# A hybrid attention layer on one core: part of the down projection by Strassen's block product, and the feed-forward casts moved to ScalarE

## The chip, the cores and the metric

The kernel runs on one core of a Trainium2 chip. A core has TensorE (PE in the profile), which multiplies matrices into the banks of PSUM, and VectorE (DVE), ScalarE (ACT), GpSimd (POOL) and SyncE (SP), each with an instruction queue of its own that is worked off in order; they meet at semaphores. The metric is the time of one execution on the device, in microseconds (us); the time told is the median of several runs.

## The reference

One layer of a streaming encoder, for 512 prompt tokens and 32 sample tokens. What matters here is its end:

```python
x = x + mixed @ w_out                        # two attention mixers, gated, [T, 1024]
h = rmsnorm(x, n2)
u = h @ w_up                                 # [T, 5632], w_up [1024, 5632]
c = conv_b + conv_w[0]*u[t-2] + conv_w[1]*u[t-1] + conv_w[2]*u[t]    # per feature, over time
a, g = split(c, 2)                           # 2816 features each
x = x + (gelu(a) * g) @ w_down               # w_down [2816, 1024]
```

The new rows of the caches (keys, values, the last two rows of `u`) are outputs too. All is float32.

## The kernel before

Activations stand transposed: features on the 128 partitions, T = 544 tokens (512 and 32) as columns, in two halves of 272. PE works on a rounded format, so each float32 operand is split into a high part (a cast) and a low part (the operand less its high part), and a product is made of three matmuls into one bank: high x high, high x low, low x high (`triple`, L210). A matmul here has a 128x128 block of weights and 272 columns.

Weights come as tiles of 128x1024 (512 KB), eight blocks each, in the order of the list `sources`: 52 tiles of `w_in`, 8 of `w_out`, 44 of `w_up`, 22 of `w_down`. `prep` (L185) loads a tile, makes its high part on POOL (L193) and its low part on DVE (L194), with two buffers for each of the three; `weights()` has it done up to three tiles ahead, at a low priority for the scheduler.

The order of PE's work is that in which Python emits it: `Stream` keeps a clock of its own while it emits, and lets attention tasks in between the projections when their operands should be there. Which instruction stands where on the other engines, and small exchanges on PE, are decided by the framework's scheduler, which goes by priorities and by its own estimate of durations. So an instruction can stand far from where the code emits it.

The feed-forward part has two stages.

- Up projection: `conv` (L921) takes tiles in pairs, a value tile `i` and its gate tile `GT + i`. Each tile is 48 matmuls (8 blocks, 2 halves, 3 products). DVE takes each half out of its bank times the norm (L925), ACT and DVE make the convolution (L931, L932, L937), POOL keeps the last rows of each sequence (L928, L929) and mends the sample's first two tokens (L934, L935) by a small table `carry`, made once by POOL (L916 to L919). ACT makes the gelu (L945), DVE multiplies by the gate (L950), and `split` (L419) makes the high part on ACT (L420) and the low part on DVE (L421) of the 22 gated tiles.
- Down projection (loop at L970): for each of 8 output tiles, 22 row blocks x 2 halves x 3 matmuls into two banks, then DVE adds the residual `x1` (L984) and SP stores the tile (L988, the last one in two halves, L986).

`fp` is a pool of 39 buffers of 128x544 and `gp` one of 19; `psd` and `psa` are 3 and 5 banks of PSUM.

Of the kernel before, what the change touches and what calls it, by code (L numbers as in the profile page):

```python
# [30 lines left out]
B_BLK = 96               # sample keys of mixer B: 3 blocks of 96 (32 new, 256 cached)
LN_EXP = "natural_log_exp_and_others"

# tiles of w_in, 128 output features each
QA, KA, VA, QB, KB, VB, GA, GB = 0, 8, 10, 12, 20, 28, 36, 44

# columns of the packed per-feature vectors
# [101 lines left out]
def body(ctx, tc, a, o):  # L139
# [39 lines left out]
    for i in range(GT):  # L179
        sources += [a["w_up"][i], a["w_up"][GT + i]]  # L180
# [789 lines left out]
    for m in range(KC):  # L970
# [5 lines left out]
        for k, s in order:  # L976
# [6 lines left out]
            if k == GT - 1:  # L983
                V.tensor_tensor(y[:, c0:c0 + cn], ps[s][:, :cn], x1[m][:, c0:c0 + cn], ALU.add)  # L984
                if tail:
                    nc.sync.dma_start(out=o["y"][m, :, c0:c0 + cn], in_=y[:, c0:c0 + cn])  # L986
# [118 lines left out]
```

## Time and profile before

| | |
|---|---|
| median of 3 runs | 934.15 us (934.09 to 934.8) |
| profiled execution: span from the first to the last instruction | 931.9 us |
| busy in the span: PE, DVE, ACT, POOL | 905.8, 656.7, 445.1, 467.0 us |
| down projection on PE | about 796 to 928.7 us |

The profile shows one execution. It gives the span and no time of its own beside it; the runs were timed apart from it. Busy time of PE counts a matmul's whole passage, and matmuls overlap (0.288 us each, started every 0.125 us), so the pace is read from the starts.

### The profile page before, as it was taken

How to read it: one execution, taken by the hardware profiler on the slowest of the kernel's cores; microseconds unless marked ns; L12 is line 12 of the kernel's file. 1: busy time of each engine (PE TensorE's matmuls, PEld its weight loads, DVE VectorE, ACT ScalarE, POOL GpSimd, SP SyncE). 2: the span in 40 equal slices, each digit the busy share in tenths (PEclk: the TensorE clock that was granted, in tenths of full speed). 3: DMA queues.
4: the chain of work that ended last, by engine and by line, in shares of the span. 5: the costliest groups of instructions: out<-in, count | busy, mean ns of one | idle time of the engine just before them, and what ended most of it. 6: DMA issues, size and time to landing. Idle time of an engine off the chain costs nothing.

```text
span 931.9 us, 18669 instructions
## 1 busy us (share of the span) xinstructions
PE 905.8 (97%) x7181; PEld 891.7 (96%) x7181; DVE 656.7 (70%) x1243; ACT 445.1 (48%) x1103; POOL 467.0 (50%) x636
## 2 busy tenths in 40 slices
PE   7979999999999999999999999999999999999998
PEld 6878999989989999999999999999999999999998
DVE  7798867777988988989766568777777777422221
ACT  5667887778878687777672232222222222000000
POOL 5625548366777677766451146544555554311110
PEclk9999999999999999999999999999999999999999
DMA  6222123312344344334324222222222222333321
GB/s 220 89 91 83 52 95 99 103 59 83 109 145 128 98 138 128 127 110 125 107 86 169 89 70 91 91 91 91 91 84 80 87 92 91 107 103 103 113 90 40
DMA packets 39000, 94.35 MB, mean 101 GB/s; under 512 B 4832, under 2 KB 14336, under 8 KB 38912
## 3 DMA queue, kind: packets, MB, share of 16 engines
q1 hardware_dynamic: 38912, 93.17, 31.1%
q8 instruction: 56, 0.92, 0.4%
q14 instruction: 32, 0.26, 0.1%
HBM read 80.48 MB, written 7.10 MB: 94 GB/s over the span
## 4 chain that ended last, share of the span: by engine, by line
PE 78%; DVE 8%; ACT 3%; POOL 3%; issue 2%; DMA 0%; DVEq 0%; POOLq 0%; ACTq 0%
PE ps L80 75%; PE ps L84 3%; DVE q L436 1%; ACT p L475 1%; DVE w_lo L194 1%; DVE p L491 1%; POOL p L483 1%; DVE zn L412 1%; DVE s L244 1%; DVE t_b L309 1%; POOL t_sql L404 1%; DVE k L421 0%; POOL z L411 0%; DVE xl L317 0%; DMA k<-k 0%
## 5 line engine op out<-in xcount | busy, mean ns | idle before, releaser
L80 PE MATMUL ps<-xh,w_lo 128*128 128x272 f32 x1536 | 444.4, 290 | 5.9 <-DVE w_lo L194 5.8
L80 PE MATMUL ps<-xh,w_hi 128*128 128x272 f32 x1536 | 444.1, 291 | 3.4 <-ACT z L402 1.6
L80 PE MATMUL ps<-xl,w_hi 128*128 128x272 f32 x1536 | 444.2, 290 | 1.3 <-DVE xl L317 1.2
L80 PEld LDWEIGHTS ps<-xh,w_lo 128*128 128x128 f32 x1536 | 289.4, 189 | 7.6 <-DVE w_lo L194 7.0
L80 PEld LDWEIGHTS ps<-xh,w_hi 128*128 128x128 f32 x1536 | 289.7, 189 | 4.9 <-ACT z L402 1.9
L80 PEld LDWEIGHTS ps<-xl,w_hi 128*128 128x128 f32 x1536 | 289.8, 189 | 2.6 <-DVE xl L317 2.1
L193 POOL TENSOR_SCALAR w_hi<-w_raw 128x1024 fp32r<-128x1024 f32 (+2 forms) x128 | 137.5, 1074 | 288.8 <-PE ps L80 178.2
L194 DVE TENSOR_TENSOR w_lo<-w_raw,w_hi 128x1024 fp32r<-128x1024 f32 (+2 forms) x128 | 162.4, 1270 | 105.6 <-POOL w_hi L193 105.2
L80 PE MATMUL ps<-s,w_hi 128*128 128x272 f32 x960 | 180.6, 288 | 0.0
L80 PEld LDWEIGHTS ps<-s,w_hi 128*128 128x128 f32 x960 | 150.4, 188 | 0.0
L80 PE MATMUL ps<-s,w_lo 128*128 128x272 f32 x480 | 137.8, 288 | 0.0
L483 POOL TENSOR_SCALAR p<-p,rc 128x256 f32<-128x256 f32 (+3 forms) x128 | 74.5, 598 | 43.3 <-DVE rc L481 39.9
L80 PEld LDWEIGHTS ps<-s,w_lo 128*128 128x128 f32 x480 | 90.2, 188 | 0.0
L475 ACT ACTIVATE p<-p,nm 128x256 f32<-128x256 f32 (+3 forms) x128 | 65.4, 513 | 27.8 <-DVE nm L472 27.7
L925 DVE TENSOR_TENSOR u<-ps,rstd 128x272 f32<-128x272 f32 x88 | 38.2, 438 | 38.8 <-PE ps L80 38.2
L420 ACT CAST s<-s 128x544 fp32r<-128x544 f32 x30 | 19.4, 647 | 84.9 <-DVE s L950 81.5
L80 PE MATMUL ps<-k,q 128*128 128x256 f32 (+2 forms) x256 | 52.1, 308 | 3.3 <-DMA k<-k 1.6
L404 POOL TENSOR_TENSOR t_sql<-t_sq,t_sqh 128x272 fp32r<-128x272 f32 x52 | 52.6, 1011 | 3.7
L411 POOL TENSOR_TENSOR z<-z,t_y 128x272 f32<-128x272 f32 x52 | 42.6, 821 | 21.9 <-ACT t_y L306 19.9
L931 ACT ACTIVATE s<-u,cols 128x544 f32<-128x544 f32 x44 | 36.9, 842 | 34.0 <-DVE u L925 34.0
L945 ACT ACTIVATE s<-s 128x544 f32<-128x544 f32 x22 | 14.5, 658 | 75.5 <-DVE s L937 75.5
L403 POOL TENSOR_SCALAR t_sqh<-t_sq 128x272 fp32r<-128x272 f32 x52 | 29.9, 575 | 39.4 <-ACT t_sq L401 34.7
(129 smaller groups left out, 1340.9 us busy)
## 6 DMA issues: line engine op xcount, KB each, us to landing
w_raw<-in_w_in SPq DMA_DIRECT2D x50, 512.0 KB, 3.3
w_raw<-in_w_up SPq DMA_DIRECT2D x44, 512.0 KB, 3.2
w_raw<-in_w_down SPq DMA_DIRECT2D x22, 512.0 KB, 3.2
k<-k SPq DMA_DIRECT2D x40, 128.0 KB, 2.3
bias<-in_rel SPq DMA_DIRECT2D x16, 256.0 KB, 2.7
w_raw<-in_w_out SPq DMA_DIRECT2D x8, 512.0 KB, 3.3
s<-in_x SPq DMA_DIRECT2D x15, 272.0 KB, 5.6
out_vb<-s SPq DMA_DIRECT2D x8, 272.0 KB, 2.3
```

What stands on the lines that cost most here:

```text
L80: return self.nc.tensor.matmul(out, lhsT=lhsT, rhs=rhs, **kw)
L84: return self.nc.tensor.transpose(out, src, ident)
L193: G.tensor_scalar(hi[:, c], raw[:, c], 1.0, 1.0, ALU.mult, ALU.mult)
L194: V.tensor_tensor(lo[:, c], raw[:, c], rr(hi)[:, c], ALU.subtract)
L403: G.tensor_scalar(sqh, sq, 1.0, 1.0, ALU.mult, ALU.mult)
L404: G.tensor_tensor(sql, sq, rr(sqh), ALU.subtract)
L411: G.tensor_tensor(z, z, y, ALU.mult)
L420: nc.scalar.copy(dst_hi, src)
L475: act(p[:, sl], p[:, sl], AF.Exp, bias=nm[:, t:t + 1], accum_out=sm[:, t:t + 1])
L483: G.tensor_scalar(p[:, sl], p[:, sl], rc[:, t:t + 1], 1.0, ALU.mult, ALU.mult)
L925: V.tensor_tensor(u[:, 2 + c0:2 + c0 + cn], ps, rstd2[:, c0:c0 + cn], ALU.mult)
L931: act(c, u[:, 0:T], AF.Identity, scale=col("cw0", m), bias=col("cb", m))
```

## The change

Of the 22 row blocks of the down projection, 6 (blocks 16 to 21, `REST`) are multiplied as before, and first: their gated tiles are now the first that the up projection makes. The other 16 make 8 pairs (block j with block j + 8). For a pair of output tiles, the 2x2 blocks of weights and the 2x2 blocks of the pair's two gated tiles (each cut into its two halves of 272 columns) are multiplied in Winograd's form of Strassen's product, with 7 products for 8:

- `make_pair` builds the seven moving operands of a pair from the two gated tiles: four additions or subtractions of 272 columns on DVE, the high parts on ACT, the low parts on DVE. Five pairs (`EARLY`) are made while the up projection goes on, three after it. The operands lie in the buffers of `gp`, `fp` (now 50), and, once the up projection has read them, in those of its moving operand (`xh`, `xl`).
- `sums` builds the seven weight operands. One load of 128x1024 holds the weight blocks of two pairs (a unit); DVE makes the four sums of 256 columns (one instruction for two of them), ACT the high parts, DVE the low parts. There are 4 pairs of output tiles x 4 units = 16 loads.
- Each of the seven products gathers 8 row blocks in a bank of its own (4 units x 2 x 3 = 24 matmuls), and `leave` adds the seven banks into the four quarters of the two output tiles: one copy on ACT, nine operations on DVE, two on POOL. Stores are by quarters.
- The high part of every weight tile of `w_up` and `w_down` is made on ACT, no longer on POOL.

```diff
-    for i in range(GT):
+    ffn = len(sources)
+    gate_order = list(range(2 * PAIRS, GT)) + [j + e * PAIRS for j in range(PAIRS) for e in range(2)]
+    for i in gate_order:
         sources += [a["w_up"][i], a["w_up"][GT + i]]
-    sources += [a["w_down"][m] for m in range(GT)]
+    sources += [a["w_down"][m] for m in range(KC * REST // 8)]
...
-            G.tensor_scalar(hi[:, c], raw[:, c], 1.0, 1.0, ALU.mult, ALU.mult)
+            if n < ffn:
+                G.tensor_scalar(hi[:, c], raw[:, c], 1.0, 1.0, ALU.mult, ALU.mult)
+            else:
+                nc.scalar.copy(hi[:, c], raw[:, c])
...
-    fp = att.enter_context(tc.tile_pool(name="fp", bufs=39, reuse_waits="tile"))
+    fp = att.enter_context(tc.tile_pool(name="fp", bufs=50, reuse_waits="tile"))
...
+    def make_pair(v1, v2):
+        b11, b12, b21, b22 = (v[:, c:c + H] for v in (v1, v2) for c in (0, H))
+        t13, t24 = (fp.tile([128, T], F32, name="s") for _ in range(2))
+        first, *wide = home(), (home(), home()), (home(), home()), (home(), home())
+        nc.scalar.copy(first[:, :H], b11)
+        V.tensor_tensor(first[:, H:], b11, rr(first)[:, :H], ALU.subtract)
+        split(*wide[0], v2)
+        V.tensor_tensor(t13[:, :H], b11, b12, ALU.subtract)
+        V.tensor_tensor(t13[:, H:], b12, b22, ALU.subtract)
+        split(*wide[1], t13)
+        V.tensor_tensor(t24[:, :H], b22, t13[:, :H], ALU.add)
+        V.tensor_tensor(t24[:, H:], b21, t24[:, :H], ALU.subtract)
+        split(*wide[2], t24)
...
+    def sums():
+        for n in range(KC // 2 * UNITS):
+            raw = wp.tile([128, 1024], F32, name="w_raw", bufs=2)
+            load(raw, a["w_pair"][n])
+            wc, wd, wa, wb = (raw[:, 256 * e:256 * e + 256] for e in range(4))
+            s13, s24 = (fp.tile([128, 2, 256], F32, name="s") for _ in range(2))
+            s1, s3, s2, s4 = s13[:, 0], s13[:, 1], s24[:, 0], s24[:, 1]
+            V.tensor_tensor(s13, raw[:, 256:768].rearrange("p (e c) -> p e c", e=2),
+                            wc.unsqueeze(1).to_broadcast([128, 2, 256]), ALU.add)
+            V.tensor_tensor(s2, s1, wa, ALU.add)
+            V.tensor_tensor(s4, s2, wb, ALU.add)
+            for x in (wa, s2, s3, s1, wb, wd, s4):
+                w = fp.tile([128, 2, 256], F32R, name="s")
+                nc.scalar.copy(w[:, 0], x)
+                V.tensor_tensor(w[:, 1], x, rr(w)[:, 0], ALU.subtract)
+                ready.append(w)
+                yield
...
+    FACTORS = ("b11", "t2", "t3", "t1", "b21", "t4", "b22")
...
+            if e == 0:
+                nc.scalar.copy(p1, ps[0])
+                G.tensor_tensor(y11, y11, p1, add)
+            elif e == 1:
+                tt(v2, ps[1], p1, sub)
+                tt(y12, y12, v2, sub)
+            elif e == 2:
+                tt(v3, ps[2], v2, add)
+                tt(y22, y22, v3, add)
+                G.tensor_tensor(y21, y21, v3, add)
+            elif e == 3:
+                tt(y22, y22, ps[3], sub)
+                tt(y12, ps[3], y12, add)
+                store(1, 1)
+            else:
+                y, r, h = ((y11, 0, 0), (y21, 1, 0), (y12, 0, 1))[e - 4]
+                tt(y, ps[e], y, add)
+                store(r, h)
...
+        for u in range(UNITS):
+            for e, name in enumerate(FACTORS):
+                w = operand(nprod)
+                nprod += 1
+                for j in range(2):
+                    xh, xl = pairs[2 * u + j][name]
+                    ks = slice(128 * j, 128 * j + 128)
+                    first, last = (u, j) == (0, 0), (u, j) == (UNITS - 1, 1)
+                    mm(ps[e], lhsT=w[:, 0, ks], rhs=xh, start=first, stop=False)
+                    mm(ps[e], lhsT=w[:, 0, ks], rhs=xl, start=False, stop=False)
+                    mm(ps[e], lhsT=w[:, 1, ks], rhs=xh, start=False, stop=last)
+                if u == UNITS - 1:
+                    leave(e)
```

`operand(n)` runs `sums` up to ten operands ahead of product `n`. The change also reserves less of SBUF for DMA descriptors (`dynamic_dma_scratch_size=1024`), which makes room for the larger pool. Up to the feed-forward part the instructions of every engine stand in the order of before, apart from two zeroings on DVE, which now come near its start, and the place shown next.

POOL, near the start of the program: `s<-s` is the running sum of squares for the first norm, `ks_lo` the low part of a cached key tile, `w_hi<-w_raw` the high part of weight tiles. Before:

```order
L332 TENSOR_TENSOR s<-s 128x544 x3
L421 TENSOR_TENSOR ks_lo<-c_k,ks_hi 64x128 x2
L193 TENSOR_SCALAR w_hi<-w_raw 128x1024 x2
L403 TENSOR_SCALAR t_sqh<-t_sq 128x272
L404 TENSOR_TENSOR t_sql<-t_sq,t_sqh 128x272
```

and now:

```order
L342 TENSOR_TENSOR s<-s 128x544 x3
L926 TENSOR_TENSOR carry<-cols 128x44 x2
L431 TENSOR_TENSOR ks_lo<-c_k,ks_hi 64x128
L928 TENSOR_TENSOR t_c<-cols 128x44
L431 TENSOR_TENSOR ks_lo<-c_k,ks_hi 64x128
L927 TENSOR_TENSOR carry<-carry,cols 128x44 x2
L929 TENSOR_TENSOR carry<-carry,t_c 128x44
L201 TENSOR_SCALAR w_hi<-w_raw 128x1024 x2
```

The six instructions that make `carry` stood just ahead of the feed-forward part; they now stand ahead of the high parts of the third and fourth weight tile of `w_in`.

DVE, behind the end of the up projection: before, the last tile's convolution, gate and low part, then weight low parts and the two evictions of each output tile:

```order
L194 TENSOR_TENSOR w_lo<-w_raw,w_hi 128x1024
L932 SCALAR_TENSOR_TENSOR s<-u_8049,cols,s 128x544
L937 SCALAR_TENSOR_TENSOR s<-u_8049,cols,s 128x544
L950 TENSOR_TENSOR s<-s 128x544
L421 TENSOR_TENSOR s<-s 128x544
L194 TENSOR_TENSOR w_lo<-w_raw,w_hi 128x1024 x2
L984 TENSOR_TENSOR s<-ps,s 128x272 x2
```

Now, from the second to the third weight low part of the six blocks (the third is the last row; L967 to L971 and L431 make the operands of late pairs, L1055 is the eviction):

```order
L965 TENSOR_TENSOR xh_11205<-s,xh_11205 128x272
L970 TENSOR_TENSOR s<-s 128x272
L967 TENSOR_TENSOR s<-s 128x272
L968 TENSOR_TENSOR s<-s 128x272
L942 SCALAR_TENSOR_TENSOR s<-u_8049,cols,s 128x544
L431 TENSOR_TENSOR xh_11167<-s,xl_11166 128x544
...
L1055 TENSOR_TENSOR s<-ps,s 128x272
L431 TENSOR_TENSOR xl_11188<-s,xh_11187 128x544
L947 SCALAR_TENSOR_TENSOR s<-u_8049,cols,s 128x544
L204 TENSOR_TENSOR w_lo<-w_raw,w_hi 128x1024
```

The weight low parts, which came back to back with the evictions, now have the late pairs' work between them.

DVE, at the change from one pair of output tiles to the next (L1014 to L1017 are the weight sums of the next unit, L1021 the low parts of its operands, L1080 to L1092 the evictions of the seven banks); before, three `w_lo` stood between two evictions here. Now:

```order
L1014 TENSOR_TENSOR s<-w_raw 128x512
L1016 TENSOR_TENSOR s<-s,w_raw 128x256
L1017 TENSOR_TENSOR s<-s,w_raw 128x256
L1080 TENSOR_TENSOR t_b<-ps,t_y 128x272
L1021 TENSOR_TENSOR s<-w_raw,s 128x256
L1021 TENSOR_TENSOR s<-s 128x256
L1081 TENSOR_TENSOR s<-s,t_b 128x272
L1083 TENSOR_TENSOR t_v<-ps,t_b 128x272
L1021 TENSOR_TENSOR s<-s 128x256 x2
L1092 TENSOR_TENSOR s<-ps,s 128x272
```

The evictions stand between the low parts that PE takes next.

## Rows read from the trace of the kernel before

**Rows 1.** The page, part 1: busy us (share of the span) x instructions.

```profile
PE 905.8 (97%) x7181; PEld 891.7 (96%) x7181; DVE 656.7 (70%) x1243; ACT 445.1 (48%) x1103; POOL 467.0 (50%) x636
```

**Rows 2.** Chain of waits from 500 us on: start us, us, what.

```profile
499.99 428.74 PE ps L80 x3420
...
928.76 0.44 DVE s L984
```

**Rows 3.** Windows (stretch; length; busy us of PE, PEld, DVE, ACT, POOL; PEclk; DMA).

```profile
640.00:680.00 40.00, 40.00 (x321) 40.00 (x321) 29.77 (x41) 9.82 (x13) 21.31 (x35) 1.00 0.26 83
800.00:840.00 40.00, 40.00 (x321) 40.00 (x320) 11.70 (x14) 0.65 (x1) 7.84 (x7) 1.00 0.32 107
```

**Rows 4.** Timeline of PE: start us, us, line, operation; three low-part matmuls.

```profile
788.03 0.28 PE L80 MATMUL ps<-xh,w_lo 128*128 128x272 f32 x1
...
811.72 0.29 PE L80 MATMUL ps<-s,w_lo 128*128 128x272 f32 x1
...
928.44 0.28 PE L80 MATMUL ps<-s,w_lo 128*128 128x272 f32 x1
```

**Rows 5.** Timeline of POOL at the start; in brackets idle us before.

```profile
19.18 1.85 POOL L421 TENSOR_TENSOR ks_lo<-c_k,ks_hi 64x128 fp32r<-64x128 f32 x2
23.69 2.56 POOL L193 TENSOR_SCALAR w_hi<-w_raw 128x1024 fp32r<-128x1024 f32 x2 [2.66 <-DVE s L332]
```

**Rows 6.** Timeline of POOL, of the six carry instructions.

```profile
483.96 1.50 POOL L916 TENSOR_TENSOR carry<-cols 128x44 f32<-128x44 f32 x2
485.43 0.28 POOL L918 TENSOR_TENSOR t_c<-cols 128x44 f32<-128x44 f32 x1
...
487.17 0.76 POOL L919 TENSOR_TENSOR carry<-carry,t_c 128x44 f32<-128x44 f32 x1
```

**Rows 7.** Timeline of all engines around 25 us.

```profile
25.27 3.19 DVE L194 TENSOR_TENSOR w_lo<-w_raw,w_hi 128x1024 fp32r<-128x1024 f32 x2
...
27.37 0.39 PE L80 MATMUL ps<-xh,w_lo 128*128 128x272 f32 x1 [1.46 <-DVE w_lo L194]
...
27.60 0.29 PE L80 MATMUL ps<-xh,w_hi 128*128 128x272 f32 x1
```

**Rows 8.** ACT's groups by shape: busy us, mean ns of one, idle before.

```profile
L420 ACT CAST s<-s 128x544 fp32r<-128x544 f32 x30 | 19.4, 647 | 84.9 <-DVE s L950 81.5 <-DVE s L818 3.2
...
L420 ACT CAST ks_hi<-c_k 128x256 fp32r<-128x256 f32 x8 | 3.2, 401 | 0.6 <-DMA c_k<-in_cb_k 0.4
```

**Rows 9.** DVE's groups by shape, 560 to 800 us (up projection).

```profile
L421 DVE TENSOR_TENSOR s<-s 128x544 fp32r<-128x544 f32 x20 | 24.3, 1217 | 0.0
```

**Rows 10.** DVE's groups by shape, 800 to 932 us (down projection).

```profile
L194 DVE TENSOR_TENSOR w_lo<-w_raw,w_hi 128x1024 fp32r<-128x1024 f32 x20 | 24.5, 1226 | 78.1 <-POOL w_hi L193 78.1
L984 DVE TENSOR_TENSOR s<-ps,s 128x272 f32<-128x272 f32 x16 | 6.5, 440 | 17.4 <-PE ps L80 17.4
...
L421 DVE TENSOR_TENSOR s<-s 128x544 fp32r<-128x544 f32 x1 | 0.7, 726 | 0.7 <-ACT s L420 0.7
```

**Rows 11.** Timeline of DVE in the up projection.

```profile
700.02 0.44 DVE L925 TENSOR_TENSOR u<-ps,rstd 128x272 f32<-128x272 f32 x1 [1.17 <-PE ps L80]
701.09 1.23 DVE L194 TENSOR_TENSOR w_lo<-w_raw,w_hi 128x1024 fp32r<-128x1024 f32 x1 [0.62 <-POOL w_hi L193]
...
706.03 0.44 DVE L925 TENSOR_TENSOR u<-ps,rstd 128x272 f32<-128x272 f32 x1 [0.85 <-PE ps L80]
706.39 1.24 DVE L421 TENSOR_TENSOR s<-s 128x544 fp32r<-128x544 f32 x1
707.56 1.22 DVE L194 TENSOR_TENSOR w_lo<-w_raw,w_hi 128x1024 fp32r<-128x1024 f32 x1
```

**Rows 12.** DVE's groups by shape, whole span: 512, 272 and 256 columns.

```profile
L421 DVE TENSOR_TENSOR k<-zn,k 64x272 fp32r<-64x272 f32 x20 | 13.2, 659 | 3.7 <-ACT k L420 3.4
...
L455 DVE TENSOR_TENSOR v<-ps,v 128x512 fp32r<-128x512 f32 x10 | 6.8, 680 | 0.4 <-ACT v L454 0.3
...
L194 DVE TENSOR_TENSOR w_lo<-w_raw,w_hi 128x256 fp32r<-128x256 f32 x2 | 0.8, 416 | 0.0
```

More of the change, by code (lines that the diff above doesn't have):

```diff
@@ L27 @@
 GT = FF // 128
+PAIRS = 8
+REST = GT - 2 * PAIRS
+EARLY = 5
+UNITS = PAIRS // 2
+H = T // 2
 EPS = 1e-6
@@ L939, in conv, with home @@
         dense(evac, psa if n % 2 else psd)
-    for i in range(GT):
+    rest, pairs = [], []
+    homes = [gp] * 19 + [fp] * (7 * EARLY + 2 * REST - 19) + [f"x{p}{k}" for k in range(KC) for p in "hl"]
+    def home():
+        h = homes.pop(0) if homes else fp
+        return xp.tile([128, T], F32R, name=h) if isinstance(h, str) else h.tile([128, T], F32R, name="s")
+    def make_pair(v1, v2):
[11 more added lines that the diff above has]
+        split(*wide[2], t24)
+        ops = {"b11": (first[:, :H], first[:, H:])}
+        for names, hl in zip((("b21", "b22"), ("t1", "t3"), ("t2", "t4")), wide):
+            for e, name in enumerate(names):
+                ops[name] = tuple(x[:, e * H:e * H + H] for x in hl)
+        pairs.append(ops)
+    late = []
+    for n, i in enumerate(gate_order):
         part = []
@@ L946, in value, with gate, operand @@
             part.append(c)
-        def gate(c, part=part, i=i):
+        def gate(c, part=part, n=n):
             v = part[0]
             V.tensor_tensor(v, v, c, ALU.mult)
-            pool = fp if i < 13 else gp
-            h = pool.tile([128, T], F32R, name="s")
-            l = pool.tile([128, T], F32R, name="s")
-            split(h, l, v)
-            gated.append((h, l))
-        conv(i, 2 * i, value)
-        conv(GT + i, 2 * i + 1, gate)
-    nc.sync.dma_start(out=o["conv"], in_=state_u)
-    blocks = [(m, k) for m in range(KC) for k in range(GT)]
+            if n < REST:
+                h, l = home(), home()
+                split(h, l, v)
+                rest.append((h, l))
+                return
+            late.append(v)
+            if n % 2 and len(pairs) < EARLY:
+                make_pair(*late)
+                late.clear()
+        conv(i, 2 * n, value)
+        conv(GT + i, 2 * n + 1, gate)
+    nc.sync.dma_start(out=o["conv"], in_=state_u)
+    for j in range(0, len(late), 2):
+        make_pair(late[j], late[j + 1])
+    def sums():
[15 more added lines that the diff above has]
+                yield
+    ready = []
+    making = sums()
+    def operand(n, ahead=10):
+        while len(ready) <= n + ahead:
+            with tc.high_priority(LATER):
+                if next(making, 0) == 0:
+                    break
+        return ready[n]
     held = {}
@@ L971, in body @@
         ps = [bank(psa if m % 2 else psd) for _ in HALVES]
-        y = fp.tile([128, T], F32, name="s")
-        tail = 8 if m == KC - 1 else 0
-        order = [(k, s) for k in range(GT - tail) for s in range(2)]
-        order += [(k, s) for s in range(2) for k in range(GT - tail, GT)]
-        for k, s in order:
-            c0, cn = HALVES[s]
-            hi, lo = block(m * GT + k)
-            gh, gl = (x[:, c0:c0 + cn] for x in gated[k])
-            mm(ps[s][:, :cn], lhsT=hi, rhs=gh, start=k == 0, stop=False)
-            mm(ps[s][:, :cn], lhsT=hi, rhs=gl, start=False, stop=False)
-            mm(ps[s][:, :cn], lhsT=lo, rhs=gh, start=False, stop=k == GT - 1)
[L983 to L986, printed above, removed]
@@ L987, in body @@
-        if not tail:
-            nc.sync.dma_start(out=o["y"][m], in_=y)
+        for k in range(REST):
+            for s, (c0, cn) in enumerate(HALVES):
+                hi, lo = block(m * REST + k)
+                gh, gl = (x[:, c0:c0 + cn] for x in rest[k])
+                mm(ps[s][:, :cn], lhsT=hi, rhs=gh, start=k == 0, stop=False)
+                mm(ps[s][:, :cn], lhsT=hi, rhs=gl, start=False, stop=False)
+                mm(ps[s][:, :cn], lhsT=lo, rhs=gh, start=False, stop=k == REST - 1)
@@ L1008, in _layout @@
     r["w_up"] = _tiles(f["w_up"][0])
-    wd = _tiles(f["w_down"][0]).reshape(KC, 128, GT, 128).transpose(0, 2, 1, 3)
+    wd = _tiles(f["w_down"][0]).reshape(KC, 128, GT, 128)
+    tail = wd[:, :, 2 * PAIRS:].transpose(0, 2, 1, 3)
     r["w_down"] = np.ascontiguousarray(
-        wd.reshape(GT, 8, 128, 128).transpose(0, 2, 1, 3).reshape(GT, 128, 1024))
+        tail.reshape(KC * REST // 8, 8, 128, 128).transpose(0, 2, 1, 3).reshape(-1, 128, 1024))
+    pair = wd[:, :, :2 * PAIRS].reshape(KC // 2, 2, 128, 2, UNITS, 2, 128)
+    r["w_pair"] = np.ascontiguousarray(
+        pair[:, ::-1].transpose(0, 4, 2, 1, 3, 5, 6).reshape(KC // 2 * UNITS, 128, 1024))
     c = np.zeros((128, NCOLS), np.float32)
```

21 lines of the change are left out of this document (20 added, 1 removed).

## The prediction

> **What bounds the kernel now.** I read the page's busy shares first: TensorE (PE) is busy for 97% of a span of 931.9 us [rows 1]. A busy PE need not be the bound, so the chain of waits came next, from 500 us on, since all that the change touches comes after that, but for six small POOL instructions and two memsets: the chain is PE from 499.99 to 928.73 us, 3420 matmuls with nothing between them, then one eviction of 0.44 us [rows 2]. So in both feed-forward stages only the number of matmuls counts, as long as nobody comes late for them. The table by windows shows that the granted clock there is 1.00, which is the 2.4 GHz level, and how much room the others have: of 40 us of the up projection VectorE (DVE) works 29.8, ScalarE (ACT) 9.8 and GpSimd (POOL) 21.3; in the down projection DVE works 11.7 and ACT 0.65 [rows 3]. The price of a matmul is read from PE's own timeline: between the low-part matmuls at 811.72 and 928.44 us lie 310 groups of three, so one takes 116.72 / 930 = 0.1255 us [rows 4].
>
> The median of the runs shown is 934.15 us, 2.25 us over the profiled span. I sum against the span and add these 2.25 us.
>
> **The matmuls.** Before, the down projection has 8 output tiles x 22 row blocks x 2 column halves x 3 products = 1056. After: six blocks in the old way, 8 x 6 x 2 x 3 = 288, and for each of 4 pairs of output tiles 4 units x 7 products x 2 row blocks x 3 = 168, so 672; in all 960. The 96 that go are worth 96 x 0.1255 = **12.05 us**, all on the path. The up projection keeps its 2112.
>
> **The start: POOL's six carry instructions.** The order shows that the scheduler moves them from a free place near 484 us to POOL's first work, around the two ks_lo subtractions and ahead of the high part of the third weight tile. Before, the ks_lo pair runs from 19.18 to 21.03 us, and then POOL idles 2.66 us until 23.69 us [rows 5]; the wait is put down to DVE, but the cast also waits for PE's last reading of the buffer that it overwrites, and PE reads that tile until about then. The six took from 483.96 to 487.93 us, 3.97 us [rows 6], while DVE was almost always busy, as it is at 20 us. Then POOL is free at 21.03 + 3.97 = 25.0 us instead of 23.69, and the cast (half of the 2.56 us for two) ends at 26.28 instead of 24.97. DVE's subtraction of that tile started at 25.27 [rows 7], when its earlier work was done, so it moves by 26.28 - 25.27 = 1.0 us, and PE, which already waits 1.46 us for it until 27.37 us [rows 7], waits as much longer. Nothing later in a PE-bound program gives that back. Bounds: 0, if each takes 0.28 us and all fit in the gap of 2.66 us, and 1.3 us, the delay of the cast itself. I take **1.0**.
>
> **The up projection.** A weight tile's high part moves from POOL (1.06 us, off everybody's way) to ACT. ACT casts 128x544 in 647 ns and 128x256 in 401 [rows 8], 0.85 ns per element, so 1024 take about 1.06 us; that is my estimate from the two rows. Four tiles take 4 x 48 x 0.1255 = 24.1 us of PE. In that time ACT had 5.9 us of work and gets 4.2 more for the weights and about 1.1 for a pair of gated tiles (three 544 casts and a 272 one for the former two): 11.2 of 24.1. DVE had 17.9; it loses two low parts of 1.22 us and gets three of 0.73 and five 272-wide operations of 0.44 [rows 9, 10]: 19.8 of 24.1. It is a matter of order, then, not of load. Now a tile's low part is made between 701.09 and 702.32 us, after an eviction that starts at 700.02 us when PE ends the tile before [rows 11]; PE needs it one tile, 6.02 us, later, so it is 3.7 us early. A pair can put up to 2.1 us of its own DVE work (one 0.73, three 0.44) in front. I charge 0; if the lead were overdrawn, each late tile would cost its lateness, with 20 tiles beside pairs.
>
> The low part of 128x544 took 1217 ns twenty times while POOL was at work, and 726 ns once it was idle [rows 9, 10], so freeing POOL helps DVE. The Trainium skill names the cause: by "GPSIMD Engine Reference", section "1. Specifications", GpSimd's path to SBUF is shared with VectorE instructions that read two SBUF tensors. The trace agrees with its 1217 against 726. By that rule the eight POOL additions of the new evictions would slow DVE in turn, which the room found below covers.
>
> **The six remaining blocks.** 288 matmuls are 36.1 us. In them DVE makes three late pairs (3 x 4.4 = 13.2 us: three low parts of 0.73 and five of 0.44 each), six weight low parts (7.4), 16 evictions (7.0), the last gated tile (2.7) and the first unit of weight sums and part of the second (6.0): 36.3 us laid end to end. But DVE starts an operation before the last one has ended: an eviction of 0.44 us starts at 706.03 and the next operation at 706.39, that one of 1.24 us is followed at 707.56 [rows 11]. So 0.07 to 0.08 us of each of some 63 go, and 31.5 remain of 36.1. The tightest place is the third weight tile of this stage, needed after 96 matmuls = 12.0 us: by the DVE order 21 operations of about 12 us stand in front of it or are it. PE has some seven high-part products to do first (0.9 us). I charge **0.2**, between 0 and 2.
>
> **The products.** A pair of output tiles takes PE 168 x 0.1255 = 21.1 us. DVE has four units of one 512-wide sum (0.68), two 256-wide sums and seven low parts (0.416 each) [rows 12], 4 x 4.42 = 17.7, and nine evictions of 0.44: 21.7 end to end, and with 49 overlaps of 0.08 us 17.8, 84% of PE's time. ACT has 28 casts of 0.40 and one copy, 11.6. The pool leaves nine slots beside the operands and x1, two of them for sums, so seven weight operands are in flight: a slot is free when PE ends a product and is needed six products, 36 x 0.1255 = 4.5 us, later. Cast and subtraction take under 1 us, so a lead of 3.5 us. At a change of tiles nine evictions fall into one unit: 3.7 + 3.2 = 6.9 us of DVE against PE's 5.3, which takes 1.6 of the 3.5. I charge 0, with the stall of the rivals below as the other bound. The evictions' first copy is on ACT and two additions on POOL, each ready well before DVE's use of them. The end is as before: one 272-wide eviction and one half store.
>
> "VectorE: DVE Perf Modes" in the Trainium skill, section "The DRAIN you can't avoid", has the next operation wait until the pipe is empty (its text lets one that is not held start earlier). The rows with 0.36 us from start to start of a 0.44 us operation speak against the strict reading here; the strict one would give the 21.7 us above.
>
> **Sum.** -12.05 + 1.0 + 0.2 = -10.85: span 921.05 us, and with the 2.25 us outside it **923.3 us**.
>
> **Rivals.**
> First, DVE is late in places: at full durations end to end the pairs take 21.7 instead of 21.1 us, 4 x 0.6 = 2.4 us, and the six blocks lose up to 2. That is 925.5 to 928; I put it at 926.5. For it speaks how full DVE gets, against it the overlap in rows 11.
> Second, and slower: DVE sets the pace of the products. The break-even lies where the stalls eat 10.85 us, 2.7 for each pair of tiles, so at 23.8 us of DVE work, 1.1 times the durations end to end. Such prices exist: a 64x272 low part in the attention took 659 ns [rows 12], 1.5 times 0.44, with POOL busy. At 1.2 times, 26.0 us a pair, the time is 923.3 + 4 x 4.9 = 943 us. Against it: POOL has only eight additions in this stage.
> Third, PE pays for waits. There are two for every product, 224 in all, where weights came 8 blocks at a time. A matmul after a real stall is followed 0.23 us later instead of 0.125 [rows 7]; at half of that excess, 0.05 each, 11 us are lost and the time is 934.5, no change. Against it: the first output tile of before waits for ACT on every sixth matmul, and from 788.03 to 811.72 us, which holds it, 63 groups took 23.69 us [rows 4], 0.1253 each matmul, no slower than the rest.
> That the change would not do what it says can be left out: the order has 96 matmuls fewer.
>
> **Chances.** Forecast 0.70 (922 to 925); first rival 0.16; second 0.07; third 0.07, half of it too small to reach no change. Faster 0.88, within 0.2% (1.9 us, about what a measurement of this kernel can tell) 0.04, slower 0.08. The range begins at 921.6, no cost at the start and half a us for the reading of the pace, and ends at 928 with the first rival.
>
> **What would show it.** 960 matmuls in the down projection at 0.125 us and the chain still all PE from 500 us; the third weight tile's cast at about 25 us and PE's wait before 27.37 us grown to about 2.5; PE waits on low parts of weight sums under 1 us in all; POOL nearly empty in the up projection and 544-wide low parts at 0.73 us. Wrong: PE idle more than 3 us after 500 us, on DVE's low parts or sums, or a pace above 0.127 us in the products.

## The result, and the profile after

| | predicted | measured |
|---|---|---|
| time | 923.3 us (921.6 to 928.0) | 923.92 us, median of 4 runs (922.2 to 924.88) |
| against the kernel before | -10.85 us | -10.55 us (before: 934.47 us, median of 4 runs beside it); ratio 0.9881, interval 0.9862 to 0.99: 9.3 to 12.9 us faster |
| profiled span | 921.05 us | 923.0 us (before 931.9 us) |

Two later measurements gave 0.9869 (0.9844 to 0.9894) and 0.9874 (0.9851 to 0.9898). The forecast came true. Of its three terms the largest was exact, the smallest was 0 instead of 0.2 us, and the one for the start came by another way than the one forecast; the base on which the sum stood was itself off. The rows show it.

The page's first part, and the chain from 500 us on, of the kernel after:

```profile
PE 898.6 (97%) x7085; PEld 884.4 (96%) x7085; DVE 723.6 (78%) x1471; ACT 542.2 (59%) x1285; POOL 379.1 (41%) x578
```
```profile
3 pieces in order of time: start us, us, what
499.94 419.80 PE ps L85 x3350
919.75 0.02 issue
919.77 0.44 DVE s L1092
```

DVE and ACT are busier than in [rows 1], POOL less, and none of that shows in the chain: as in [rows 2], PE runs without a wait up to the last eviction. The table by windows (span of the window, PE, PEld, DVE, ACT, POOL busy, granted clock, DMA share, GB/s) answers to [rows 3]; the second stretch lies in the six remaining blocks, the third and fourth in the products.

```profile
640.00:680.00 40.00, 40.00 (x321) 40.00 (x320) 30.07 (x47) 16.33 (x21) 10.08 (x28) 1.00 0.29 93
800.00:836.00 36.00, 36.00 (x289) 36.00 (x288) 28.79 (x58) 11.98 (x21) 2.21 (x4) 1.00 0.27 91
857.00:878.00 21.00, 21.00 (x170) 21.00 (x168) 19.60 (x52) 10.68 (x30) 1.66 (x2) 1.00 0.39 127
878.00:899.00 21.00, 21.00 (x170) 21.00 (x169) 19.32 (x53) 10.36 (x30) 1.93 (x2) 1.00 0.47 153
```

The clock is at its 2.4 GHz level throughout. DVE has 28.8 of 36 us to do beside the six blocks, and 19.3 to 19.6 of 21 in the middle of the products. How long a pair of output tiles takes is read from POOL's first addition of each: the starts are 21.06 and 21.02 us apart, and 168 x 0.1255 is 21.1.

```profile
873.70 0.78 POOL L1078 TENSOR_TENSOR s<-s,t_y 128x272 f32<-128x272 f32 x1 [17.76 <-ACT t_y L1077]
...
894.76 0.77 POOL L1078 TENSOR_TENSOR s<-s,t_y 128x272 f32<-128x272 f32 x1 [18.00 <-ACT t_y L1077]
...
915.78 0.77 POOL L1078 TENSOR_TENSOR s<-s,t_y 128x272 f32<-128x272 f32 x1 [17.34 <-ACT t_y L1077]
```

To see what the feed-forward part alone gained, I need a mark that both traces share behind the unquiet start. The first 512-wide product of a certain value mix, which waits 0.27 or 0.28 us for its low part `pt_l`, will do. On PE's timeline it stands here, in the kernel before and in the kernel after:

```profile
370.50 0.51 PE L80 MATMUL ps<-pt_l,v 128*128 128x512 f32 x1 [0.28 <-DVE pt_l L502]
```
```profile
373.64 0.50 PE L85 MATMUL ps<-pt_l,v 128*128 128x512 f32 x1 [0.27 <-DVE pt_l L512]
```

From the mark to the end of the span the kernel before takes 931.9 - 370.50 = 561.4 us and the kernel after 923.0 - 373.64 = 549.4: 12.0 us less, against the 12.05 for 96 matmuls. But the mark itself comes 3.1 us later. That is the part before 370 us, where the change moves only POOL's six small instructions and two zeroings. There POOL, DVE and PE now read, answering to [rows 5] and [rows 7]:

```profile
18.81 1.48 POOL L926 TENSOR_TENSOR carry<-cols 128x44 f32<-128x44 f32 x2
20.25 0.93 POOL L431 TENSOR_TENSOR ks_lo<-c_k,ks_hi 64x128 fp32r<-64x128 f32 x1
21.15 0.75 POOL L928 TENSOR_TENSOR t_c<-cols 128x44 f32<-128x44 f32 x1
21.98 0.97 POOL L431 TENSOR_TENSOR ks_lo<-c_k,ks_hi 64x128 fp32r<-64x128 f32 x1
23.03 0.88 POOL L927 TENSOR_TENSOR carry<-carry,cols 128x44 f32<-128x44 f32 x2
23.87 0.28 POOL L929 TENSOR_TENSOR carry<-carry,t_c 128x44 f32<-128x44 f32 x1
24.11 2.52 POOL L201 TENSOR_SCALAR w_hi<-w_raw 128x1024 fp32r<-128x1024 f32 x2
```
```profile
24.24 1.48 DVE L352 TENSOR_TENSOR s<-s 128x544 fp32r<-128x544 f32 x1 [0.71 <-ACT s L351]
25.65 3.19 DVE L204 TENSOR_TENSOR w_lo<-w_raw,w_hi 128x1024 fp32r<-128x1024 f32 x2
```
```profile
25.21 0.40 PE L85 MATMUL ps<-xh,w_hi 128*128 128x272 f32 x1 [0.43 <-POOL w_hi L201]
...
27.76 0.40 PE L85 MATMUL ps<-xh,w_lo 128*128 128x272 f32 x1 [1.46 <-DVE w_lo L204]
...
28.39 0.43 PE L85 MATMUL ps<-xh,w_hi 128*128 128x272 f32 x1
28.62 0.43 PE L85 MATMUL ps<-xl,w_hi 128*128 128x272 f32 x1
```

In this profile the inputs landed 0.4 us earlier than before (POOL's pair of `ks_lo` would begin at 18.81, not 19.18), and yet PE reaches the third tile's low part at 27.76 instead of 27.37. The 1.46 us wait has kept its size; a new one of 0.43 us stands ahead of it, for the high part. DVE begins the low part at 25.65 without a wait for the cast: what it comes after is the addition L352, which took 1.48 us here, where POOL's first cast begins 0.13 us ahead of it, and 0.77 in the kernel before (at 24.57 us), where that cast began 0.88 us ahead. Behind these waits PE falls to the 1.2 GHz level: starts are 0.23 us apart from 28.39 us on. The windows show it there and twice more (granted clock 0.57):

```profile
28.00:30.00 2.00, 2.00 (x12) 2.00 (x12) 2.00 (x5) 0.35 (x2) 0.00 (x0) 0.58 0.58 182
30.00:32.00 2.00, 2.00 (x11) 2.00 (x11) 2.00 (x8) 0.80 (x2) 0.32 (x1) 0.57 0.90 252
69.00:73.00 4.00, 3.92 (x19) 3.92 (x20) 4.00 (x14) 3.56 (x11) 0.00 (x0) 0.57 0.61 183
110.00:114.00 4.00, 4.00 (x22) 4.00 (x22) 3.70 (x10) 2.84 (x9) 0.79 (x1) 0.57 0.12 49
```

So the question for the experiments: do the six instructions cost 3 us in the end, through a longer wait and the clock behind it, or does the start wander anyway? And which part of the change brought the 12 us?

### The profile page after: what moved, and what is told of

Its sections match the earlier page's. It is cut to its first block, busy times and chain, and to the rows that moved or that the text cites. A ratio compares the mean times of both kernels' runs of the same rounds, so it can differ in the third digit from the quotient of the medians.

```text
span 923.0 us, 18908 instructions
## 1 busy us (share of the span) xinstructions
PE 898.6 (97%) x7085; PEld 884.4 (96%) x7085; DVE 723.6 (78%) x1471; ACT 542.2 (59%) x1285; POOL 379.1 (41%) x578
## 4 chain that ended last, share of the span: by engine, by line
PE 76%; DVE 9%; ACT 4%; POOL 3%; issue 2%; DMA 0%; DVEq 0%; POOLq 0%
PE ps L85 73%; PE ps L89 3%; ACT p L485 2%; DVE q L446 1%; DVE zn L422 1%; DVE p L501 1%; DVE w_lo L204 1%; POOL p L493 1%; DVE s L254 1%; DVE t_b L319 1%; DVE k L431 1%; POOL t_sql L414 1%; POOL z L421 1%; DVE pt_l L512 0%; DMA k<-k 0%
## 5 line engine op out<-in xcount | busy, mean ns | idle before, releaser
L204 DVE TENSOR_TENSOR w_lo<-w_raw,w_hi 128x1024 fp32r<-128x1024 f32 (+2 forms) x112 | 143.2, 1279 | 30.8 <-ACT w_hi L203 18.3
L201 POOL TENSOR_SCALAR w_hi<-w_raw 128x1024 fp32r<-128x1024 f32 (+2 forms) x62 | 66.6, 1075 | 90.2 <-PE ps L85 70.3
L203 ACT CAST w_hi<-w_raw 128x1024 fp32r<-128x1024 f32 x50 | 52.6, 1051 | 64.9 <-issue 36.1
L85 PE MATMUL ps<-s,w_hi 128*128 128x272 f32 x448 | 84.0, 288 | 0.0
L938 POOL TENSOR_SCALAR state_u<-u 128x2 f32<-128x2 f32 x44 | 17.1, 388 | 148.7 <-DVE u L935 148.7
L85 PE MATMUL ps<-s 128*128 128x272 f32 (+1 forms) x483 | 71.3, 293 | 1.7 <-DVE s L372 1.7
L85 PEld LDWEIGHTS ps<-s,w_hi 128*128 128x128 f32 x448 | 70.1, 188 | 0.0
L85 PEld LDWEIGHTS ps<-s 128*128 128x128 f32 x483 | 65.1, 190 | 2.2 <-DVE s L372 1.7
L85 PE MATMUL ps<-s,w_lo 128*128 128x272 f32 x224 | 63.8, 288 | 0.0
L512 DVE TENSOR_TENSOR pt_l<-ps,pt_h 128x512 fp32r<-128x512 f32 (+1 forms) x80 | 45.6, 602 | 5.5 <-ACT pt_h L511 4.4
```

The costliest lines, as they stand in the source:

```text
L85: return self.nc.tensor.matmul(out, lhsT=lhsT, rhs=rhs, **kw)
L201: G.tensor_scalar(hi[:, c], raw[:, c], 1.0, 1.0, ALU.mult, ALU.mult)
L203: nc.scalar.copy(hi[:, c], raw[:, c])
L204: V.tensor_tensor(lo[:, c], raw[:, c], rr(hi)[:, c], ALU.subtract)
L512: V.tensor_tensor(l[:, :n], ps[:, :n], rr(h)[:, :n], ALU.subtract)
L938: G.tensor_scalar(state_u[:, m, 0:2], u[:, NP:NP + 2], 1.0, 1.0, ALU.mult, ALU.mult)
```

## The experiments

Times are compared inside one job, that is with the kernel before as it ran beside them: median 935.19 us (23 runs) for `after_again`, `carry_late`, `before_carry_early` and `casts_only`; 935.93 (13) for `carry_more`, `pairs4`, `early3` and `low_twice`; 936.02 (17) for the other four. For each kernel I also give, from its profile, the mark (start of the 512-wide product) and the stretch from it to the end of the span. That stretch hardly varies: 561.4 us in both profiles of the kernel before, 549.2 to 549.4 in three of the kernel after.

| kernel | time, us (runs) | ratio to before (interval) | mark | mark to end |
|---|---|---|---|---|
| before_again | 936.38 (12) | 1.0004 (0.9989 to 1.0018) | 373.42 | 561.4 |
| after_again | 923.77 (5) | 0.9869 (0.9844 to 0.9894) | 372.68 | 549.2 |
| after_third | 923.52 (6) | 0.9874 (0.9851 to 0.9898) | 372.52 | 549.2 |
| carry_late | 921.24 (4) | 0.9853 (0.9828 to 0.9878) | 369.79 | 549.2 |
| carry_late_again | 923.37 (4) | 0.9868 (0.9842 to 0.9895) | 371.60 | 549.3 |
| before_carry_early | 934.27 (12) | 0.9994 (0.998 to 1.0008) | 373.39 | 560.3 |
| carry_more | 924.95 (4) | 0.9888 (0.987 to 0.9907) | 373.32 | 549.3 |
| casts_only | 933.69 (12) | 0.9988 (0.9975 to 1.0002) | 370.37 | 561.3 |
| casts_pool | 924.81 (6) | 0.9881 (0.9857 to 0.9904) | 375.20 | 549.2 |
| pairs4 | 929.88 (4) | 0.9944 (0.9924 to 0.9964) | 372.45 | 555.7 |
| early3 | 924.44 (4) | 0.9883 (0.9862 to 0.9904) | 373.59 | 549.4 |
| low_twice | 937.56 (10) | 1.0017 (0.9999 to 1.0034) | 375.48 | 563.2 |

**after_again, carry_late, before_carry_early: the start.** `carry_late` keeps the six behind the last high part that POOL makes for the output projection; `before_carry_early` gives their tiles a place that is free from the start. The first edit is on the kernel after (`state["hi"]` is that last cast), the second on the kernel before:

```diff
+    with tc.issue_after(state["hi"].ins):
+        for r in range(2):
+            G.tensor_tensor(carry[:, :, r], per("cw0"), state_c[:, :, r], ALU.mult)
...
```
```diff
-    carry = ft.tile([128, UT, 2], F32, name="carry")
+    carry = const.tile([128, UT, 2], F32, name="carry")
...
-    t = ft.tile([128, UT], F32, name="t_c")
+    t = const.tile([128, UT], F32, name="t_c")
```

> The changed kernel once more, beside the other three. Its first runs gave 923.92 us (922.2 to 924.88) at granted clocks of 0.993 to 0.998, where the sum had 923.3; in its profile the stretch up to the last up-projection eviction is 3.3 us longer than before and the rest 12.2 us shorter. Theory (the start): the six carry instructions make PE's wait at 25 us longer and PE falls to the 1.2 GHz level behind it, so the profile again shows half-clock stretches before 120 us and 923 to 924.5 us. Rival (scatter): the half-clock stretches come and go by chance, and the time wanders between 921 and 925.

> The changed kernel with the six carry instructions back behind the last high part of the output projection on POOL, as before; nothing else moves. The sum: 1.0 us less than the changed kernel, 922.3 us. Theory (the start): the wait before the third weight tile is 1.46 us at 27.4 us again and no half-clock stretch follows it, so 921.5 to 922.5 us, about 12 us under the kernel before, with the up projection's first eviction within 0.5 us of the former 543.3 us. Rival (scatter): the carry instructions are worth 0.4 us and the half-clock stretches turn up all the same: 923.5 us, the first eviction at 545 to 547 us.

> The kernel before with the same six instructions moved to POOL's start (their two small tiles in the constants' pool), nothing else: the start's price without the rest of the change. The sum has 1.0 us: 935.4 us. Theory (the start): 0.4 to 0.8 us of longer wait and up to 1.5 to 2.7 us of half clock, 935.3 to 937.5 us. Rival (scatter): 934.5 to 935.0 us, and half-clock stretches no more frequent than in the kernel before.

`carry_late` against `after_again` looked like the theory (2.5 us), `before_carry_early` against it (no change: 934.27 against 935.19 us). Half-clock stretches turned up in `carry_late` all the same (granted clock 0.68 from 16 to 20 us, 0.50 from 68 to 72), and `before_carry_early` has both waits but none behind them (starts 0.12 to 0.13 us apart). The traces say what the six do at their own place. In `carry_late` and in `before_carry_early` the inputs land within 0.05 us of each other (POOL's next work begins at 19.27 and 19.30), and PE reaches the third tile's low part here, in this order:

```profile
27.55 0.39 PE L85 MATMUL ps<-xh,w_lo 128*128 128x272 f32 x1 [1.46 <-DVE w_lo L204]
```
```profile
25.70 0.39 PE L80 MATMUL ps<-xh,w_hi 128*128 128x272 f32 x1 [0.43 <-POOL w_hi L193]
...
28.25 0.39 PE L80 MATMUL ps<-xh,w_lo 128*128 128x272 f32 x1 [1.47 <-DVE w_lo L194]
```

The price there is 0.70 us less those 0.03: 0.67 us. DVE's timelines show where it arises, in the same order:

```profile
24.64 0.88 DVE L352 TENSOR_TENSOR s<-s 128x544 fp32r<-128x544 f32 x1 [0.71 <-ACT s L351]
25.44 3.19 DVE L204 TENSOR_TENSOR w_lo<-w_raw,w_hi 128x1024 fp32r<-128x1024 f32 x2
```
```profile
24.73 1.49 DVE L342 TENSOR_TENSOR s<-s 128x544 fp32r<-128x544 f32 x1 [0.71 <-ACT s L341]
26.14 3.20 DVE L194 TENSOR_TENSOR w_lo<-w_raw,w_hi 128x1024 fp32r<-128x1024 f32 x2
```

The addition ahead of the low part starts 0.09 us later and takes 0.61 us more: the first of POOL's two casts begins 0.12 us ahead of it (24.61 us), not 0.75 (23.89), so that it lies beside more of it. The low part itself waits for no cast. (That `before_carry_early` is 1.1 us shorter behind the mark I followed only in part: a wait of 0.35 us that the kernel before has at 398.87 us, for a low part, is not there.) What became of it later, this job left open: the profiles with the six early reached the mark later, but the timed runs of the kernel before spread over 6.7 us.

**before_again, after_third, carry_late_again: the control.** No edits.

> The kernel before, run as one of the kernels that are compared, as a control: two jobs gave it spans from 930.3 to 937.7 us, wider than any of the others. Theory (its own first 370 us wander by that much): a median within 0.5 us of the kernel before it is compared with, spans again spread over 5 us or more. Rival (only the reference runs are longer, by their place in the job): 1 to 1.5 us faster than the kernel before, spans within 3 us.

> The changed kernel a third time, beside the next. Theory (the start): its profile reaches the first 512-wide product of the value mix, at 370.5 us in the kernel before, at 372.4 us or later, as all seven profiles with the carry instructions early did (372.4 to 375.5); time 923 to 924.5 us. Rival (scatter): the profile reaches it at 370 to 372 us.

> The changed kernel with the six carry instructions late, again, with nothing else moved. Theory (the start): the profile reaches the first 512-wide product of the value mix at 371 us or earlier, as the three profiles with them late did (369.8 to 370.5), and the time is 1 to 2.5 us under the changed kernel beside it. Rival (scatter): the two kernels' times agree within 0.7 us.

No single pair of kernels settles the theory of the start. `before_again`, with the six late, reached the mark at 373.42, in the middle of the kernels with them early (372.45 to 375.48); its 12 runs had spans of 931.9 to 935.9 us, 4 apart where 5 or more were expected. `after_third` ran at a granted clock of 1.00 all through, with no half-clock stretch, and still came to the mark at 372.52. `carry_late_again` came to it at 371.60, later than the theory allowed, and differs from `after_third` by 0.15 us; in the two jobs the kernel with the six late is 2.5 and 0.2 us ahead. The start wanders from run to run: the spans are 919.1 to 926.9 us in 15 runs of the kernel after and 930.3 to 937.7 in 65 of the kernel before. A part of that goes with the clock: of these 65, the five at a mean granted clock of 1.00 average 931.9 us, the 18 at 0.993 or less 934.6.

All runs together say more. The span of each is on record, and the stretch behind the mark belongs to the kernel, so span less stretch is an estimate of when each run came to the mark. In each job the kernels with the six early come out later on average: 372.3 against 371.3 us (17 and 39 runs), 373.2 against 372.3 (12 and 13, without `low_twice`), 373.6 against 372.5 (12 and 33). Together that is 1.0 us, with a 95% interval of 0.4 to 1.6; by medians the differences are 1.5, 0.7 and 0.0. This estimate was made after the fact, over kernels that differ in more than the six, with stretches from single profiles, so it supports a cost of about 1 us and does not show it as a test made for it would.

**carry_more: more POOL work at the same place.**

```diff
+    for u in us:
+        G.tensor_tensor(u[:, 2:2 + NCOLS], cols, cols, ALU.mult)
     for r in range(2):
         G.tensor_tensor(carry[:, :, r], per("cw0"), state_c[:, :, r], ALU.mult)
```

> The changed kernel with two more GpSimd instructions of 128x312 at the start, beside the six (their results are overwritten), and two of the six behind the third weight tile's high part: some 2.3 us more and 0.6 us less ahead of it, 1.7 us net. Theory (the start is on the path: a later high part makes PE wait as much longer and nothing gives it back): PE's wait before the third tile's low part grows from 1.46 to about 3 us, and the time by 1.7 us, to 925.5 us. Rival (the start's waits are taken up by later ones, so that it doesn't matter): the wait grows, the time stays at 923.8 us within 0.7.

The cast of the third tile began at 24.75 us, 0.6 later than in the kernel after, and the low part did not follow: PE took it at 27.64, its wait down to 0.20 us, with two other waits (1.51 and 0.77) ahead of it. (More moved than POOL's work: PE's products with `ones` now all stand ahead of this tile's high parts, so this is no clean test of a later cast.) POOL's timeline of this kernel, and VectorE's:

```profile
24.75 1.04 POOL L201 TENSOR_SCALAR w_hi<-w_raw 128x1024 fp32r<-128x1024 f32 x1
25.76 0.74 POOL L929 TENSOR_TENSOR carry<-carry,cols 128x44 f32<-128x44 f32 x1
26.48 2.02 POOL L201 TENSOR_SCALAR w_hi<-w_raw 128x1024 fp32r<-128x1024 f32 x1
```
```profile
26.29 1.30 DVE L204 TENSOR_TENSOR w_lo<-w_raw,w_hi 128x1024 fp32r<-128x1024 f32 x1
```

The reason is beside it: here the low part began 0.19 us ahead of POOL's next cast and took 1.30 us; in the kernel after it began at 25.65, with that cast under way, and PE got it 2.1 us later. Here the cast paid, with 2.02 us (1.26 on average for the two in the kernel after). So a later cast does not move PE by as much; DVE and POOL share the delay between them. Time: 924.95 us against 923.5 to 923.9 in other jobs, between the two expectations, which it does not tell apart.

**casts_only and casts_pool: the two parts of the change apart.** The first puts this into the kernel before, the second takes it out of the kernel after.

```diff
+    ffn = len(sources)
...
-            G.tensor_scalar(hi[:, c], raw[:, c], 1.0, 1.0, ALU.mult, ALU.mult)
+            if n < ffn:
+                G.tensor_scalar(hi[:, c], raw[:, c], 1.0, 1.0, ALU.mult, ALU.mult)
+            else:
+                nc.scalar.copy(hi[:, c], raw[:, c])
```

> The kernel before with the feed-forward weights' high parts cast on ScalarE instead of GpSimd (66 tiles), down projection as before. The sum charges 0 for it: 934.5 us within 0.5, low parts of the weights in the up projection at about 1.2 us as before and those of the gated 128x544 tiles at 0.73 us instead of 1.22. Rival (GpSimd's work slows VectorE where PE waits): 1 to 3 us faster. Rival (ScalarE late with the high parts): slower by 1 us or more, with PE waits for a cast in the up projection.

> The changed kernel with the feed-forward weights' high parts back on GpSimd (50 tiles of 1.06 us), Strassen as it is: the other part of the change alone. The sum gives the casts 0: 923.8 us within 0.7, like the changed kernel. Theory (a shared way into memory only costs VectorE room that it has): the low parts of 128x544 tiles at 1.2 us instead of 0.73, no PE wait after 400 us, the same 549.3 us from the first 512-wide product of the value mix to the end. Rival (GpSimd's casts make VectorE late beside the six remaining blocks): 2 us or more longer from there, with PE waits for low parts between 800 and 840 us.

The casts are worth nothing either way: 561.3 from the mark to the end beside 561.4, and 549.2 beside 549.2. The times alone would not say so: `casts_only` is 1.5 us under the kernel before (ratio 0.9988, with 1 inside the interval), and `casts_pool` 0.3 over its expected range; behind the mark neither differs. The groups of DVE by form between 560 and 800 us (count, total and mean ns, idle before), of the kernel after and of `casts_pool`, show that the low parts did get dearer with POOL at work, 989 ns for 721 (1.2 us were expected):

```profile
L431 DVE TENSOR_TENSOR s<-s 128x544 fp32r<-128x544 f32 x21 | 15.1, 721 | 2.9 <-ACT s L430 2.9
```
```profile
L428 DVE TENSOR_TENSOR s<-s 128x544 fp32r<-128x544 f32 x21 | 20.8, 989 | 2.9 <-ACT s L427 2.9
```

DVE had the room, in the up projection and beside the six blocks (31.06 us busy of 36 there, for 28.79), and PE had no wait after the mixing. Strassen's part made all of the 12 us.

**pairs4: half of Strassen.**

```diff
-PAIRS = 8
+PAIRS = 4
```

> The changed kernel with 8 row blocks by Strassen and 14 in the old way, instead of 16 and 6: 672 + 336 = 1008 matmuls, 48 more than the changed kernel and 48 fewer than before. Theory (each matmul removed is worth 0.1255 us and nothing else is on the path): 6.0 us slower than the changed kernel, 929.8 us against its 923.8, and the stretch from 370 us to the end 6.0 us longer. Rival (the products cost PE a little at each of their waits, which the removed matmuls outweigh): with half the products the price halves too, so under 5.5 us.

About 6.1 us slower than the kernel after (929.88 against 923.5 to 923.9 in the other jobs), and 6.3 us longer from the mark, of which 6.0 lie before PE's last matmul; the rest is DVE, late with the last evictions: a pair of output tiles has half the products there and as many evictions, and the chain that ended last runs through DVE from 910 us on. Each matmul is worth its 0.1255 us, at 1056, 1008 and 960 of them: up to PE's last matmul the two steps of 48 are 6.1 and 6.0 us.

**early3: two more pairs beside the six blocks.**

```diff
-EARLY = 5
+EARLY = 3
```

> The changed kernel with three pairs of gated tiles made in the up projection and five beside the six remaining blocks, instead of five and three: two pairs, some 2 x 3.8 us of VectorE, move into a stretch of 36.1 us where it had 31.5 us to do. Theory (work there is free until its consumer waits; the last pairs are read only in the fourth unit, 16 us into the products): 0 to 1 us slower, 923.8 to 925 us. Rival (VectorE fills the stretch, 39 of 36.1 us, and the weights' low parts behind it come late): 3 us slower, with PE waits for low parts between 800 and 850 us.

549.4 us from the mark: nothing. DVE was busy for 32.07 of 36 us there (28.79 with five early) and no product waited.

**low_twice: where VectorE sets the pace.**

```diff
-            for x in (wa, s2, s3, s1, wb, wd, s4):
+            for e, x in enumerate((wa, s2, s3, s1, wb, wd, s4)):
...
-                V.tensor_tensor(w[:, 1], x, rr(w)[:, 0], ALU.subtract)
+                for _ in range(1 + (e % 4 > 0)):
+                    V.tensor_tensor(w[:, 1], x, rr(w)[:, 0], ALU.subtract)
```

> The changed kernel with five of the seven low parts of the weight sums made twice (the second writes the same values): 80 more 128x256 instructions on VectorE in the products, 20 for each pair of output tiles. The changed kernel's VectorE was busy 51.1 of the 63 us at its end, 17.1 of the 21.1 us of a pair. Theory (what VectorE does counts at the start-to-start price, 0.34 us, and costs nothing until it passes PE's time): 17.1 + 6.8 = 23.9 us a pair, 2.8 over, so 4 x 2.8 = 11 us slower less up to 3.5 of lead: 931 to 935 us, PE waiting for low parts from the first pair on. Rival (VectorE counts at full durations end to end): 21.7 + 8.3 = 30.0 us a pair, 36 us slower: 955 to 960 us. Rival (waits of PE come first, VectorE has far more room than it shows): under 2 us slower.

Five of the seven low parts of a unit (e is 1, 2, 3, 5 or 6) are made twice. 13.9 us longer from the mark, 3 to 7 more than the theory and less than half of the strict rival's 31 to 36. The theory's kind was right: VectorE's work counts by starts, and past PE's time it sets the pace. Its number was missed. PE's waits from 836 us on (total us, times, longest):

```profile
PE ps L85 <- DVE s L1022: 5.3, 7, 2.4
PE ps L85 <- DVE s L1093: 1.0, 1, 1.0
PE ps L85 <- DVE t_v L1084: 0.5, 1, 0.5
```

That is 6.8 us. Behind the longest wait PE falls to the 1.2 GHz level for a while (granted clock 0.79 from 885 to 890 us, 0.87 to 895), and matmuls behind waits start 0.23 to 0.25 us apart; how the rest of the 13.9 us divides I did not work out. Two things were missing in the theory. Its base of 17.1 us a pair was too small: it came from 860 to 923 us, with the kernel's idle end. The rows of 857 to 899 us above have 19.3 to 19.6, and 6.8 more would be 26.1 to 26.4, where 25.2 were measured. The other is POOL. Its timeline shows 4.18 us twice for an addition that takes 0.88 in the kernel after, and DVE's timeline a quarter of the output that waits for it:

```profile
858.60 4.18 POOL L1086 TENSOR_TENSOR s<-s,t_v 128x272 f32<-128x272 f32 x1 [3.10 <-DVE t_v L1084]
...
884.59 4.18 POOL L1086 TENSOR_TENSOR s<-s,t_v 128x272 f32<-128x272 f32 x1 [4.04 <-DVE t_v L1084]
```
```profile
861.48 0.68 DVE L1014 TENSOR_TENSOR s<-w_raw 128x512 f32<-128x512 f32 x1
862.81 0.44 DVE L1093 TENSOR_TENSOR s<-ps,s 128x272 f32<-128x272 f32 x1 [0.66 <-POOL s L1086]
```

The chain that ended last runs through the first of the two additions; what they cost apart from DVE's work no run shows.

By POOL's first additions (854.49, 879.32, 905.09, 930.05) a pair now takes 25.2 us, and there the whole gain is gone: 937.56 us, no better than before.

## Why the prediction was right, point by point

**What bounds it.** Right: no wait of PE after 500 us, the chain is PE.

**The matmuls, -12.05.** Exact: 561.4 less 549.2 to 549.4 is 12.0 to 12.2 us, and pairs4 shows it linear. The pace stayed under the 0.127 us that would have been a sign of being wrong.

**The start, +1.0.** The size fits, the way there does not. The forecast had DVE's low part wait for the end of POOL's later cast, and PE for it. In the traces the low part waits for no cast; it is the addition ahead of it that takes 0.6 us more, now that it starts with the cast, and PE is late by 0.67. The gap between POOL's `ks_lo` and the cast is overrun by 0.7 us, not 1.31, because the six took 3.5 us there (19.30 to 24.61 in `before_carry_early`, less 1.85 for `ks_lo`) and not the 3.97 of [rows 6]. The row that I said would show it was wrong as well: the wait at 27.4 us did not grow to 2.5, a new one appeared before it. Over all runs the kernels with the six early come to the mark some 1.0 us later (0.4 to 1.6, the estimate above), near the forecast, but that the two numbers meet is partly luck: the forecast priced one wait, and the estimate holds whatever else the six change up to the mark. And "nothing later in a PE-bound program gives that back" is too strong for this part of the program, which is not PE-bound: the same VectorE instructions of the softmax came 1.93 us later than before at 68.94 us and only 0.69 later at 88.19, since a wait for PE that was 1.69 us before is 0.72 now. Before and after:

```profile
67.01 0.34 DVE L491 CUSTOM_DVE_ANT_0 p<-ps,bias,cols 128x128 f32<-128x128 f32 x1
...
87.50 0.48 DVE L491 CUSTOM_DVE_ANT_0 p<-ps,bias,cols 128x256 f32<-128x256 f32 x1 [1.69 <-PE ps L80]
```
```profile
68.94 0.35 DVE L501 CUSTOM_DVE_ANT_0 p<-ps,bias,cols 128x128 f32<-128x128 f32 x1
...
88.19 0.49 DVE L501 CUSTOM_DVE_ANT_0 p<-ps,bias,cols 128x256 f32<-128x256 f32 x1 [0.72 <-PE ps L85]
```

**The base.** I summed against one profile, span 931.9 us, mark at 370.50. `before_again` had 934.8 and 373.42 with the same work behind the mark, and the spans of the kernel before have medians of 933.1 to 933.9 us in the three later jobs, so the base was from the fast end of a start that wanders. In 11 of the 15 runs of the kernel after the span came out 0.2 to 2 us over the predicted 921.05, in one 5.9 over. The 2.25 us outside the span were mis-sized too, as a median less the span of another run: run by run it is 2.07 to 2.17 in the kernel before and 1.74 to 1.92 in the kernel after. The median is 1.77 to 1.87 in all other changed kernels but pairs4 (2.14); no run shows why. The two errors partly cancel in 923.3.

**The up projection, 0.** Right. ACT's cast of 128x1024 took 1.05 us (1.06 estimated), the 544-wide low parts 0.72 (0.73), and DVE was busy 30.1 of 40 us. POOL, forecast as nearly empty there, still worked 10.1 of 40.

**The six blocks, +0.2.** It was 0, and there is room for two more pairs (early3). DVE's time laid by starts, 31.5 us, was the right account and, if anything, too much (28.8 of 36 us busy).

**The products, 0.** Right, with less room than forecast. VectorE was busy 70.5 us from 836 to 920 us, 17.6 a quarter, but that stretch holds only 14 of the 16 units' sums and 105 of the 112 low parts; with the rest, some 5 us laid by starts, a pair comes to about 18.9 us by my estimate, and the two in the middle have 19.6 and 19.3, where 17.8 were predicted. All of it is under PE's 21.1, so nothing was lost.

**The rivals.** The first, DVE late in places, did not come. The second exists about where it was worked out: I put the break-even at 23.8 us of DVE work a pair; low_twice, which ran at 25.2, was just past it. The third, a price for each of 224 waits, is refuted by pairs of 21.02 to 21.06 us.

## What to carry to other kernels

Where the chain is PE alone, a cut in matmuls is worth count times pitch to the tenth of a microsecond, and the work that pays for it on other engines is free as long as its time laid by starts stays under PE's. Measure such a change from a mark behind the unquiet part of a program: whole spans of these kernels wander by 7 us, the stretch behind the mark by 0.2. A small delay in such an unquiet part can't be priced from one profile or one pair of kernels; many timed runs, less the fixed stretch behind the mark, narrow it down.

## What the runs showed of the hardware

A GpSimd addition with two inputs (128x272) took 0.77 to 1.15 us in the kernel after, and up to 4.18 us in `low_twice`. VectorE's busy share alone does not tell the two apart: it was also full around the addition of 0.88 us at 855.05 in the kernel after, whose price shows on VectorE (two low parts took 1.33 us there, and 0.75 at 874.35). Both times that the addition took 4.18 us, VectorE ran ten operations with two inputs in SBUF back to back (to 862.16 and 888.15 us), and the addition ended 0.62 us behind the last of them. With POOL's casts beside them VectorE's 544-wide low parts took 989 or 1217 ns instead of 721. The Trainium skill ("Trainium Architecture — The Big Picture", section "What this means for kernel authors") calls the port pair of the two an exclusive lock and not a bandwidth split; the 4.18 us fit that, but no run here tells a lock from a split. The half-clock stretches of PE in the first 120 us came and went between runs of one kernel (granted clock 0.993 to 1.00). Of the three profiles of the kernel after, the one without any came first to the mark, but only 0.16 us ahead of one with two.
